# A hybrid decoder layer on one core: attention with a written order on the matmul engine

## The chip, the core and the metric

The kernel runs on one core of a Trainium2 chip. A core has five engines that run beside each other and meet through semaphores: PE (TensorE, matrix products into the accumulator PSUM; PEld is its loading of the stationary operand), DVE (VectorE), ACT (ScalarE), POOL (GpSimdE) and SP (SyncE, which here issues the DMAs). The metric is device time in microseconds (us) of one execution, lower is better.

## The reference

One layer: two mixers read the same normalized input, their outputs go through one output projection, and a convolutional feed-forward part follows. Cut to the mixer that the change touches:

```python
xn = rms_norm(h, mix_pre_g[l])
proj = xn @ w_in[l]                       # z | xbc | dt | q | k | v
...
y_ssd = ssd_mixer(z, xbc, dt_raw, ...)
y_sb = rms_norm(stick_breaking_attention(q, k, v).reshape(Bsz, L, SB_WIDTH), sb_norm_g[l])
mix = jnp.concatenate([y_ssd, y_sb], axis=-1) @ w_out[l]
h = h + rms_norm(mix, mix_post_g[l])
# feed-forward: up projection, causal convolution of 3, gelu gate, down projection

# stick_breaking_attention, for a block of 128 queries i of one head
zlog = jnp.einsum('bqhd,bkhd->bhqk', qi, kp) * scale
log_beta = jax.nn.log_sigmoid(zlog)
log_keep = jnp.where(valid, log_beta - zlog, 0.0)
after = lax.cumsum(log_keep, axis=3, reverse=True) - log_keep
w = jnp.where(valid, jnp.exp(log_beta + after), 0.0)
return jnp.einsum('bhqk,bkhd->bqhd', w, vp)
```

Sixteen heads of 64, 1024 tokens behind 16 learned meta tokens (L = 1040), model width 1024, all float32.

## The kernel before

The program goes through four stages: the SSD mixer (to about 440 us), attention (440 to 1048 us), the output projection with its norms, and the feed-forward part (from about 1205 us). The change is in the second.

**Attention** runs over eight pairs of heads (`p`) and, in each pair, eight blocks of 128 queries (`i`). A block of index i sees 16 + 128(i+1) keys, so its work grows with i. One block takes these steps, in this order of need:

- `block_weights`: the scores. PE multiplies q by k into PSUM (`z`, L577) in one piece for i up to 2, in two for i from 3 to 6 and in three for i = 7. ACT takes two sigmoids of each piece (`kp` L578, `bt` L579). DVE forms the running product along the keys by a scan, one for each head (L582). POOL multiplies it into `bt` (L584).
- `block_turn`: PE transposes the weights in `bt`, 128 keys at a time (`tw`, L598), into one PSUM tile, or two for i from 4 on. DVE masks the diagonal part and copies the first tile to SBUF (`th`, L602 and L605); ACT copies the second (L607).
- `block_mix`: PE multiplies `th` by the values v (`av`, L619); ACT puts the result away.

`z` and `tw` come from one ring of two PSUM tiles (tag `zz`, two buffers): a new `z` or `tw` has to wait until the tile two places earlier was read, by the sigmoids (of a `z`) or by the copies (of a `tw`). After each pair, `edge_turn` and `edge_mix` do the same for the 16 keys at the end of every block's range (`twc`, `thc`, `avc`).

Between the blocks PE has other work to fill in. `qkv_steps` projects the next pair's q, k and v: nine chains of 24 matmuls (`pj`, L164) in three column pieces, with operands split into a high and a low part, hence three matmuls for each of the eight slices of the model width. `post` then turns v (`vtp`, `vtc`). Once the projections are used up, in pairs 6 and 7, `wout_steps` loads and splits eight slices of the output weights (`wora`; ACT `woha` L705, DVE `wola` L706, and a small matmul `halo` L696 of each), and `ssd_half` multiplies the SSD result by them in 16 chains (`mo`, L747, `first` in the code). When attention has ended, the second half of the output weights (`worb`) is loaded in the same way beside what remains of those chains.

**What sets the order.** In attention the order of each engine's instructions is chosen by the framework's scheduler, which starts from the order of the code and its own estimate of when things are ready. The loop at the end of attention (L773 to L806) writes for a block: scores of block b, transposes of block b-1, one chain of projection, values of block b-1. An engine works through its own list strictly in that order, so an instruction whose input is late holds up all that stand behind it. DMAs stand in SP's list in the same way.

Of the kernel before, what the change touches and what calls it, by code (L numbers as in the profile page):

```python
# [16 lines left out]
P = 128  # L17
# [3 lines left out]
NM = 16  # L21
# [30 lines left out]
def tile_layer(ctx: ExitStack, tc: tile.TileContext, x, meta, rows, parts,  # L52
# [105 lines left out]
    def project_steps(w, ncol, xh, xl, chunks, evac, name):  # L158
        hi, lo = w
        for c0, n in chunks:  # L160
            acc = psum_mm(f"pj_{name}_{c0}")
            for k in range(KB):
                for j, (a, b) in enumerate(((hi, xh), (hi, xl), (lo, xh))):
                    mm(acc[:ncol, :n], a[:, k, :ncol], b[:, k, c0:c0 + n],  # L164
                       start=(k == 0 and j == 0), stop=(k == KB - 1 and j == 2))
            evac(acc, c0, n)
            yield
# [5 lines left out]
    def flow(items, lag=1):  # L173
        post = None
        for steps, after in items:
            for i, _ in enumerate(steps):
                if i == lag and post is not None:
                    post()
                    post = None
                yield  # L180
            if post is not None:
                post()
            post = after
        if post is not None:
            post()
# [47 lines left out]
    def qkv_steps(p):  # L233
        q = rp.tile([P, L + 3], F32, tag="rq", name=f"q{p}")
        k = rp.tile([P, L], F32, tag="rk", name=f"k{p}")
        for wsrc, dst, nm in ((w_q[p], q, "q"), (w_k[p], k, "k")):
# [3 lines left out]
            yield from project_steps(load_w(wsrc, P, f"{nm}{p}"), P, xh, xl, CH, ev, f"{nm}{p}")  # L240
# [8 lines left out]
        yield from project_steps(load_w(w_v[p], P, f"v{p}"), P, xh, xl, CH, evv, f"v{p}")  # L249

        def post():
            for part in range(2):
                tp = psum_tp(f"vtp{p}_{part}")
                for b in range(4):
                    c0 = (4 * part + b) * P
                    nc.tensor.transpose(tp[:, b, :], vt[:, c0:c0 + P], ident)
                nc.vector.tensor_copy(v[:, 4 * part:4 * part + 4, :], tp)
# [11 lines left out]
        posts[p] = post  # L269

    posts = {}

    def qkv_flow(p):
        return (qkv_steps(p), lambda: posts.pop(p)())
# [13 lines left out]
    with tc.tile_pool(name="ssd", bufs=1, side="right") as sp:  # L288
        def xbc_steps(b, dst, nm):
            raw = rp.tile([P, L + 3], F32, tag="rq", name=f"craw_{nm}")  # L290
# [25 lines left out]
        def bc_flow(g):  # L316
# [4 lines left out]
            return [(xbc_steps(8 + g, bt, f"B{g}"), lambda: to_tokens(bt, bn, f"B{g}")),  # L321
                    (xbc_steps(10 + g, ct, f"C{g}"), None)]

        def x_flow(g, b):
            xsT = rp.tile([P, L], F32, tag="rk", name=f"xsT{g}_{b}")
# [8 lines left out]
            return xbc_steps(4 * g + b, xsT, f"X{g}{b}"), post  # L334
# [10 lines left out]
        def xz_flow(g):  # L345
            for b in range(4):
                yield x_flow(g, b)
            for b in range(4):
                yield z_steps(g, b), None
# [38 lines left out]
        e, s, s2, q, adt = (t3(n, tdp) for n in ("e1", "s1", "s2", "q1", "adt"))  # L388
# [35 lines left out]
        bc[0][1]()  # L424
        run(fill)

        def chunk_weights(g, c):
# [25 lines left out]
            cbm = sp.tile([P, P], F32, tag="cbm", name=f"cbm{nm}", bufs=2)  # L453
# [81 lines left out]
        run(flow([x_flow(0, b) for b in range(2, 4)] + [(z_steps(0, b), None) for b in range(4)], 2))  # L535
# [5 lines left out]
        fill = flow(qkv_flow(p) for p in range(2))  # L541
# [20 lines left out]
    def block_weights(p, i):  # L562
# [10 lines left out]
        for ci, (a, w) in enumerate(chunks):  # L573
            z = psum_zz(f"z{nm}_{ci}")
# [11 lines left out]
        return p, i, bt  # L586
# [65 lines left out]
    def attend_meta():  # L652
        mv = ap.tile([P, 2, 4, P], F32, tag="th", name="meta_v", bufs=2)[:NM].rearrange("p h b c -> p (h b) c")
# [99 lines left out]
    def ssd_half(w):  # L753
        ys = [split_y(wp, 0, 1, ("whi", "wlo", WB))]
# [16 lines left out]
    later = flow(qkv_flow(p) for p in range(2, 8))  # L771
    meta_steps = attend_meta()
    for p in range(8):  # L773
        for i in range(NT):
            turn.append(block_weights(p, i))
            if len(turn) > 1:
                mix.append(block_turn(*turn.pop(0)))
            if p == 0:
                run(fill, 1)
            elif p < 7:  # L780
                run(later, 1 + (p < 7 and i == (0 if p == 6 else NT - 1)))
            else:
                if i == 0:
                    run(later)
                elif i < 4:
                    run(meta_steps, 1)
                run(first, (0, 0, 1, 1, 1, 2, 2, 2)[i])
            if mix:
                block_mix(*mix.pop(0))
            if p == 0 and i == 2:  # L790
                token_rstd(r_ssd, ap, "a")
            if p > 0 and i == 0:
                edge = edge_turn(p - 1)
            elif p > 0 and i == 1:
                edge_mix(p - 1, edge)
        if p == 0:
            run(fill)
        if p == 6:
            xpool.close()
            w1pool = wo1.enter_context(tc.tile_pool(name="wo1", bufs=1, side="left"))  # L800
            wres = []
            halo = psum_mm("halo0")
            run(wout_steps(w1pool, 0, ssd_g, wres, halo_y(w1pool, 0, ssd_g), halo))
            halo_store(w1pool, 0, halo)
            first = ssd_half(wres)
    while turn:  # L806
        block_mix(*block_turn(*turn.pop(0)))
    edge_mix(7, edge_turn(7))
    run(meta_steps)
    apool.close()  # L810
# [796 lines left out]
```

## Time and profile before

| what | value |
|---|---|
| median of 3 timed runs | 1871.89 us (1871.78 to 1872.38) |
| the profiled execution, its own time | 1875.09 us |
| its span from first to last instruction | 1873.4 us |
| DVE busy | 1100.6 us (59%) |
| ACT busy | 761.1 us (41%) |
| POOL busy | 854.6 us (46%) |

The profiled execution is one of its own, 3.2 us above the median; 1.7 us of its time lie outside the span. The busy time of an engine is the sum of its instructions' times in the span; PE's is shown below. The ends of matmuls are modelled by the profiler, so that a chain of matmuls overlaps itself in the rows. A window row gives, for one stretch, its length and each engine's busy time; the difference is the engine's idle time there.

### The profile page before, as it was taken

What the parts mean: (1) busy time and instruction counts of PE and PEld (TensorE: products, weight loads), DVE (VectorE), ACT (ScalarE), POOL (GpSimd) and SP (SyncE); (2) the same over time, 40 slices, a digit from 0 to 9 for tenths busy, and PEclk for the clock granted to TensorE, in tenths of its full rate; (3) what the DMA queues carried; (4) which work ended last, traced back from release to release, by engine and by line L of the source; (5) the groups of instructions that cost most, each with busy time, mean ns of one, the idle gap of its engine ahead of it and who ended that gap; (6) DMA issues with size and microseconds to landing.
All of it is one profiled execution on the core that took longest, in us unless ns stands there. A gap on an engine that the chain in (4) does not pass through costs nothing. (4 is left out here: it accounts for less than half of the span.)

```text
span 1873.4 us, 27435 instructions
## 1 busy us (share of the span) xinstructions
PE 1770.0 (94%) x10957; PEld 1509.8 (81%) x10957; DVE 1100.6 (59%) x1286; ACT 761.1 (41%) x1275; POOL 854.6 (46%) x614
## 2 busy tenths in 40 slices
PE   5899999999899999999889999899999999999997
PEld 4899889888678778778647677798988999888886
DVE  5551873674645445454533336767666666666888
ACT  5323553543343444443444234443333323334444
POOL 3213663485455554554434313248777777600001
PEclk9999999999999999999979999999999999999999
DMA  4123343131011011010042355323322323187334
GB/s 151 46 69 127 80 121 115 47 99 52 12 35 35 24 34 35 23 35 24 13 131 68 119 163 186 127 70 105 111 85 85 124 98 102 66 275 252 97 114 162
DMA packets 91443, 173.96 MB, mean 93 GB/s; under 512 B 11722, under 2 KB 36714, under 8 KB 91316
## 3 DMA queue, kind: packets, MB, share of 16 engines
q1 hardware_dynamic: 91316, 172.21, 29.0%
q8 instruction: 86, 1.41, 0.3%
q14 instruction: 41, 0.34, 0.1%
HBM read 122.39 MB, written 49.79 MB: 92 GB/s over the span
## 5 line engine op out<-in xcount | busy, mean ns | idle before, releaser
L584 POOL TENSOR_TENSOR bt<-bt,kp 128x256 f32<-128x256 f32 (+7 forms) x128 | 212.7, 1681 | 238.0 <-DVE kp L582 238.0
L582 DVE TENSOR_TENSOR_SCAN kp<-kp,hold 128x272 f32<-128x272 f32 (+7 forms) x128 | 175.4, 1409 | 182.2 <-ACT kp L578 110.1
L972 POOL TENSOR_TENSOR wl<-wr,wh 128x1024 fp32r<-128x1024 f32 x44 | 109.4, 2496 | 40.7 <-ACT wh L971 40.7
L1420 PE MATMUL dn<-dl,dh 128*128 128x512 f32 x308 | 119.9, 389 | 0.1
L1420 PE MATMUL dn<-dh 128*128 128x512 f32 x308 | 119.9, 389 | 0.0
L1420 PE MATMUL dn<-dh,dl 128*128 128x512 f32 x308 | 119.8, 389 | 0.0
L1466 POOL TENSOR_TENSOR fms<-fms,nhalf 128x1 f32<-128x1 f32 x8 | 8.5, 1061 | 225.8 <-DMA ar<-fda 186.0
L598 PE MATMUL tw<-ident,bt 128*128 128x128 f32 x576 | 82.2, 281 | 21.5 <-issue 13.9
L619 PE MATMUL av<-th,v 128*64 128x128 f32 x1152 | 81.4, 282 | 19.3 <-DVE th L605 19.2
L578 ACT ACTIVATE kp<-z 128x288 f32<-128x288 f32 (+6 forms) x112 | 82.8, 739 | 37.7 <-PE z L577 35.4
L598 PEld LDWEIGHTS tw<-ident,bt 128*128 128x128 f32 x576 | 63.4, 143 | 41.9 <-issue 28.0
L619 PEld LDWEIGHTS av<-th,v 128*64 128x64 f32 x1152 | 63.3, 138 | 39.6 <-DVE th L605 26.6
L1349 ACT ACTIVATE dh<-ar 128x512 fp32r<-128x512 f32 x77 | 48.7, 632 | 111.7 <-PE dn L1420 89.2
L971 ACT ACTIVATE wh<-wr 128x1024 fp32r<-128x1024 f32 x44 | 46.6, 1060 | 114.9 <-PE fX L1029 68.3
L1101 DVE SCALAR_TENSOR_TENSOR ga<-gr,pp,ga 128x1024 f32<-128x1024 f32 x44 | 71.3, 1621 | 34.8 <-ACT ga L1094 34.0
L577 PE MATMUL z<-k,q 64*128 64x144 f32 (+6 forms) x448 | 87.0, 489 | 3.2 <-ACT bt L579 3.2
L579 ACT ACTIVATE bt<-z 128x288 f32<-128x288 f32 (+6 forms) x112 | 83.1, 742 | 0.0
L1350 DVE TENSOR_TENSOR dl<-ar,dh 128x512 fp32r<-128x512 f32 x77 | 53.2, 691 | 42.0 <-ACT dh L1349 41.9
L1420 PEld LDWEIGHTS dn<-dl,dh 128*128 128x128 f32 x308 | 57.8, 188 | 12.5 <-DVE dl L1350 0.4
L1420 PEld LDWEIGHTS dn<-dh 128*128 128x128 f32 x308 | 57.8, 188 | 12.1 <-ACT dh L1349 0.3
L1420 PEld LDWEIGHTS dn<-dh,dl 128*128 128x128 f32 x308 | 57.8, 188 | 12.0
L164 PE MATMUL pj_v<-xh,wh_v 128*128 128x346 f32 (+1 forms) x192 | 65.5, 341 | 0.0
(545 smaller groups left out, 5797.4 us busy)
## 6 DMA issues: line engine op xcount, KB each, us to landing
wr<-in_w_up SPq DMA_DIRECT2D x44, 512.0 KB, 4.5
fds<-ga SPq DMA_DIRECT2D x44, 256.0 KB, 2.0
b<-in_w_down SPq DMA_DIRECT2D x44, 256.0 KB, 5.1
ar<-fds SPq DMA_DIRECT2D x44, 256.0 KB, 2.7
fda<-ga SPq DMA_DIRECT2D x33, 256.0 KB, 3.3
ar<-fda SPq DMA_DIRECT2D x33, 256.0 KB, 3.2
yk<-yd SPq DMA_DIRECT2D x16, 512.0 KB, 3.8
zd<-zt SPq DMA_DIRECT2D x8, 520.0 KB, 3.2
```

The source lines that it names most:

```text
L164: mm(acc[:ncol, :n], a[:, k, :ncol], b[:, k, c0:c0 + n], start=(k == 0 and j == 0), stop=(k == KB - 1 and j == 2))
L577: mm(z[:, j, :w], q[h, t0:t0 + P], k[h, a:a + w], start=True, stop=True)
L578: nc.scalar.activation(kp[:, :, a:a + w], z[:, :, :w], AF.Sigmoid, scale=-QSCALE)
L579: nc.scalar.activation(bt[:, :, a:a + w], z[:, :, :w], AF.Sigmoid, scale=QSCALE)
L582: nc.vector.tensor_tensor_scan(kp[:, j][:, ::-1], kp[:, j][:, ::-1], hold[:, L - n:L][:, ::-1], 1.0, op0=ALU.mult, op1=ALU.max)
L584: nc.gpsimd.tensor_tensor(bt[:, j, 0:m], bt[:, j, 0:m], kp[:, j, 1:m + 1], op=ALU.mult)
L598: nc.tensor.transpose(tw[:, j, b, :], bt[:, j, c0:c0 + P], ident)
L619: mm(av[halves[j], :], v[:, kb, halves[j]], th[:, j, b, :], start=kb == 0, stop=kb == i)
L972: nc.gpsimd.tensor_tensor(l, raw, h.bitcast(F32), op=ALU.subtract)
L1101: nc.vector.scalar_tensor_tensor(v, self.g[jj][:, :, i:i + 256], fconv_w[:, j, i:i + 1], v, op0=ALU.mult, op1=ALU.add)
L1350: sub(lo[:, k], raw, hi[:, k].bitcast(F32), op=ALU.subtract)
L1420: mm(banks[t], u[:, 0, c], v[:, 1, :], start=(p == 0 and i == 0), stop=(p == NPR - 1 and i == 2))
```

## The change

The order of PE's instructions in attention is now the order of the code (`manual_schedule` for PE alone); the other engines keep the scheduler. The loop over the blocks is rewritten for it:

- For block b the code writes: the first two pieces of its scores, one or two half chains of projection, its third piece if it has one, the values of block b-3, the transposes of block b-2, and another half chain. Before it was scores of b, transposes of b-1, a whole chain, values of b-1.
- A projection chain yields in its middle (`halves_`), so that one step is 12 matmuls and not 24. All eight pairs' projections come from one `flow`; a pair's weights are loaded one projection ahead (`weights_of`), and the three parts of `post` are spread over three steps.
- The edge products come at blocks 2 and 3 of the next pair, not 0 and 1.
- The projections end in pair 6, block 3. The loading of `wora` is spread over blocks from pair 6, block 5, two slices for a block, and the `mo` chains start in pair 7, block 2; 13 of 16 chains now stand ahead of the end of attention or right behind it, 9 before.
- Buffers: q and k three deep, `bt` three deep and not four, the mask tile `cbm` of the SSD scan one deep and not two, two temporaries of the SSD stage share memory with others, `meta_v` moved to another pool.

```diff
     def project_steps(w, ncol, xh, xl, chunks, evac, name, halves_=False):
...
             for k in range(KB):
+                if halves_ and k == KB // 2:
+                    yield
...
+    qkv_w = [(src[p], f"{nm}{p}") for p in range(8) for nm, src in (("q", w_q), ("k", w_k), ("v", w_v))]
+    ready = {}
+
+    def weights_of(name, ahead=0):
+        n = [nm for _, nm in qkv_w].index(name) + ahead
+        if n < len(qkv_w) and qkv_w[n][1] not in ready:
+            src, nm = qkv_w[n]
+            ready[nm] = load_w(src, P, nm)
+        return ready.get(name)
+
+    def qkv_block(name, evac, halves_):
+        w = weights_of(name)
+        for i, _ in enumerate(project_steps(w, P, xh, xl, CH, evac, name, halves_)):
+            if halves_ and i == 1:
+                weights_of(name, 1)
+            yield
...
+        post += [lambda: turn_v(0), lambda: turn_v(1), turn_edge]
...
-        btt = ap.tile([P, 2, L], F32, tag="bt", name=f"bt{nm}", bufs=4)
+        btt = ap.tile([P, 2, L], F32, tag="bt", name=f"bt{nm}", bufs=3)
...
         for ci, (a, w) in enumerate(chunks):
+            if ci == 2:
+                yield
             z = psum_zz(f"z{nm}_{ci}")
...
-        return p, i, bt
+        turn.append((p, i, bt))
...
+    pe_order = ExitStack()
+    pe_order.enter_context(tc.manual_schedule(engines={mybir.EngineType.PE}))
     for p in range(8):
         for i in range(NT):
-            turn.append(block_weights(p, i))
-            if len(turn) > 1:
-                mix.append(block_turn(*turn.pop(0)))
-            if p == 0:
+            if p == 0 and i == 0:
                 run(fill, 1)
-            elif p < 7:
-                run(later, 1 + (p < 7 and i == (0 if p == 6 else NT - 1)))
...
+            block = block_weights(p, i)
+            next(block, None)
+            if p > 0 and i == 3:
+                edge_mix(p - 1, edge)
+            run(fill, 1 + (i < 3))
+            run(first, int(p == 7 and i > 4))
+            run(block)
             if mix:
                 block_mix(*mix.pop(0))
+            if len(turn) > 2:
+                mix.append(block_turn(*turn.pop(0)))
+            run(fill, int(p > 0 or i > 3))
+            if p == 6 and i == 5:
+                run(fill)
+                xpool.close()
...
+                wsteps = wout_steps(w1pool, 0, ssd_g, wres, halo_y(w1pool, 0, ssd_g), halo)
+            if p == 7 and i == 1:
+                run(wsteps)
+                halo_store(w1pool, 0, halo)
+                first = ssd_half(wres, ys1)
+            elif p > 5:
+                run(wsteps, 2)
...
+            run(first, int(p == 7 and i > 1))
...
+            if p > 0 and i == 2:
                 edge = edge_turn(p - 1)
...
+    while turn or mix:
+        if mix:
+            block_mix(*mix.pop(0))
+        if turn:
+            mix.append(block_turn(*turn.pop(0)))
+        run(first, 1)
+    edge = edge_turn(7)
+    run(first, 1)
+    edge_mix(7, edge)
     run(meta_steps)
+    pe_order.close()
```

**What stands where.** PE before, pair 3, from the scores of block 6 to those of block 7 (a name's first number is the block, a second one the piece; matmuls of the projection are `pj`, of which two are shown and the others left out):

```order
L577 MATMUL z_6_0_6223<-k_5207,q_5206 128x456 x2
L577 MATMUL z_6_1_6228<-k_5207,q_5206 128x456 x2
L164 MATMUL pj_v_0_6266<-xh,wh_v_6261 128x348
L164 MATMUL pj_v_0_6266<-xl,wh_v_6261 128x348
L598 MATMUL tw_5_0_6238<-ident,bt_5_6151 128x128 x8
...
L598 MATMUL tw_5_1_6249<-ident,bt_5_6151 128x128 x4
...
L619 MATMUL av_5_6292<-th_5_0_6247,v_5634 64x128 x8
L619 MATMUL av_5_6292<-th_5_1_6254,v_5634 64x128 x4
L577 MATMUL z_7_0_6308<-k_5207,q_5206 128x348 x2
L577 MATMUL z_7_1_6313<-k_5207,q_5206 128x348 x2
```

The same place now, with twelve `pj` at each of the two marks:

```order
L599 MATMUL z_6_0_6337<-k_5029,q_5028 128x456 x2
L599 MATMUL z_6_1_6342<-k_5029,q_5028 128x456 x2
...
L282 MATMUL vtc_6368<-ident,edge_6365 128x128
L641 MATMUL av_3_6375<-th_3_0_6313,v_5429 64x128 x8
L620 MATMUL tw_4_0_6385<-ident,bt_4_6194 128x128 x8
L620 MATMUL tw_4_1_6396<-ident,bt_4_6194 128x128 x2
...
L599 MATMUL z_7_0_6416<-k_5029,q_5028 128x348 x2
L599 MATMUL z_7_1_6421<-k_5029,q_5028 128x348 x2
```

Transposes and values between the scores of blocks 6 and 7 are those of blocks 4 and 3 now, and were both those of block 5; the values no longer stand behind their own transposes.

DVE before, same pair (`kp` the scan of both heads, `th` the copy and the mask of a `tw`):

```order
L582 SCALAR_TENSOR_TENSOR kp_6_6221<-kp_6_6221,hold 128x912 x2
L605 COPY th_5_0_6247<-tw_5_0_6238 128x1024
L602 TENSOR_TENSOR th_5_1_6254<-tw_5_1_6249,late 128x2x128
L582 SCALAR_TENSOR_TENSOR kp_7_6306<-kp_7_6306,hold 128x1040 x2
L605 COPY th_6_0_6337<-tw_6_0_6328 128x1024
L602 TENSOR_TENSOR th_6_1_6346<-tw_6_1_6339,late 128x2x128
```

DVE now:

```order
L604 SCALAR_TENSOR_TENSOR kp_6_6335<-kp_6_6335,hold 128x912 x2
L283 COPY vc_6054<-vtc_6368 128x128
L627 COPY th_4_0_6394<-tw_4_0_6385 128x1024
L624 TENSOR_TENSOR th_4_1_6399<-tw_4_1_6396,late 128x2x128
L604 SCALAR_TENSOR_TENSOR kp_7_6414<-kp_7_6414,hold 128x1040 x2
L627 COPY th_5_0_6470<-tw_5_0_6461 128x1024
L624 TENSOR_TENSOR th_5_1_6477<-tw_5_1_6472,late 128x2x128
```

The copies are those of one block earlier than before, and still stand behind the scan of the block whose scores were last written. By the ring of two, `z_7_0` of the row above reuses the tile of `tw_4_0`, and `z_0_0` of the next pair that of `tw_5_0`: they wait for these copies. Before, it was `av_5` that waited for `th_5_0`.

DVE now at the handover from projections to output weights, pair 6, blocks 6 and 7:

```order
L627 COPY th_4_0_8222<-tw_4_0_8213 128x1024
L624 TENSOR_TENSOR th_4_1_8227<-tw_4_1_8224,late 128x2x128
L728 SCALAR_TENSOR_TENSOR wola_8232<-wora_8229,pp,woha_8231 128x1024
L728 SCALAR_TENSOR_TENSOR wola_8240<-wora_8237,pp,woha_8239 128x1024
L728 SCALAR_TENSOR_TENSOR wola_8301<-wora_8298,pp,woha_8300 128x1024
L604 SCALAR_TENSOR_TENSOR kp_7_8245<-kp_7_8245,hold 128x1040 x2
L627 COPY th_5_0_8288<-tw_5_0_8279 128x1024
L624 TENSOR_TENSOR th_5_1_8295<-tw_5_1_8290,late 128x2x128
L728 SCALAR_TENSOR_TENSOR wola_8309<-wora_8306,pp,woha_8308 128x1024
```

And PE there, block 7 and the start of pair 7:

```order
L718 MATMUL halo_8168<-wora_8229,y_8169 2x512 x2
L599 MATMUL z_7_0_8247<-k_6848,q_6847 128x348 x2
L599 MATMUL z_7_1_8252<-k_6848,q_6847 128x348 x2
L599 MATMUL z_7_2_8257<-k_6848,q_6847 128x344 x2
L641 MATMUL av_4_8267<-th_4_0_8222,v_7250 64x128 x8
L641 MATMUL av_4_8267<-th_4_1_8227,v_7250 64x128 x2
L620 MATMUL tw_5_0_8279<-ident,bt_5_8128 128x128 x8
L620 MATMUL tw_5_1_8290<-ident,bt_5_8128 128x128 x4
L718 MATMUL halo_8168<-wora_8237,y_8169 2x512 x2
L718 MATMUL halo_8168<-wora_8298,y_8169 2x512 x2
L599 MATMUL z_0_0_8318<-k_7455,q_7454 128x144 x2
```

From the last `pj` on, in pair 6, block 3, seven blocks stand on PE with nothing between them but the small `halo` matmuls and the turning of v, until the first `mo` chain in pair 7, block 2. Before, projections filled PE to the end of pair 6.

More of the change, by code (lines that the diff above doesn't have):

```diff
@@ L793, in tile_layer @@
                 edge = edge_turn(p - 1)
[L794 to L805, printed above, removed]
```

98 lines of the change are left out of this document (47 added, 51 removed).

## The prediction

> **What bounds the kernel now.** I read the page first: each engine's busy time and the clock strip.
>
> ```profile
> PE 1770.0 (94%) x10957; PEld 1509.8 (81%) x10957; DVE 1100.6 (59%) x1286; ACT 761.1 (41%) x1275; POOL 854.6 (46%) x614
> PEclk9999999999999999999979999999999999999999
> ```
>
> PE is busy 94% of the span and the next engine 59%, so the time is PE's work, plus its idle stretches, plus what a lower clock adds. The strip dips in one slice, in attention's second half. The change leaves the matmuls alone; it can only win or lose idle time and clock. So the windows view comes next, one row for each pair of heads and finer rows about the dip (columns: window, length, busy time and count of PE, PEld, DVE, ACT, POOL, granted clock, DMA share, GB/s).
>
> ```profile
> 440.60:507.90 67.30, 58.49 (x427) 47.08 (x426) 35.11 (x43) 27.66 (x47) 39.74 (x38) 0.99 0.09 28
> 507.90:572.80 64.90, 60.27 (x462) 49.40 (x460) 32.51 (x38) 29.39 (x51) 33.80 (x30) 0.98 0.08 26
> ...
> 643.90:715.00 71.10, 66.56 (x507) 55.22 (x505) 35.48 (x43) 29.95 (x52) 37.70 (x30) 1.00 0.10 31
> ...
> 786.10:857.40 71.30, 66.48 (x505) 55.17 (x503) 35.39 (x43) 29.95 (x52) 37.61 (x30) 1.00 0.10 31
> 857.40:930.30 72.90, 66.94 (x506) 55.37 (x503) 37.95 (x44) 27.66 (x50) 31.21 (x26) 1.00 0.05 16
> 930.30:953.80 23.50, 18.38 (x135) 8.60 (x131) 16.69 (x25) 13.05 (x20) 6.51 (x11) 1.00 0.47 141
> 953.80:974.30 20.50, 17.28 (x62) 10.99 (x63) 7.20 (x11) 10.29 (x20) 11.55 (x12) 0.50 0.31 101
> 974.30:985.40 11.10, 11.10 (x57) 8.58 (x57) 0.00 (x0) 3.49 (x6) 2.60 (x2) 1.00 0.41 138
> 985.40:1047.60 62.20, 60.18 (x379) 45.80 (x377) 24.23 (x20) 21.03 (x33) 26.84 (x15) 1.00 0.17 57
> 1047.60:1101.00 53.40, 49.58 (x219) 34.61 (x217) 16.05 (x13) 19.09 (x23) 10.50 (x4) 0.94 0.51 156
> ```
>
> A pair in the steady part (pairs 2 to 5; the third row shown is pair 3, the fourth pair 5) takes 71.1 us with PE idle for 4.5. Pair 0 is idle for 8.8. From 857.4 to 1047.6, where projections give way to output weights, the idle times are 6.0, 5.1, 3.2, 0 and 2.0, together 16.3. Of 17.28 us busy at clock 0.50, half, 8.6, is the price of the clock. What ends the idle time of pair 3 is in the waits view for PE in that window (us in total, times, longest):
>
> ```profile
> PE av L619 <- DVE th L605: 1.7, 3, 1.0
> PE tw L598 <- issue: 1.5, 3, 0.6
> PE tw L598 <- POOL wl_k L154: 0.8, 1, 0.8
> PE z L577 <- ACT bt L579: 0.5, 1, 0.5
> ```
>
> These are small stalls: values that wait for a copy, transposes that wait for sigmoids (the ring). They understate a little. The timeline shows a chain's matmuls starting 0.16 us apart:
>
> ```profile
> 639.71 0.32 PE L164 MATMUL pj_v<-xh,wh_v 128*128 128x346 f32 x1
> ...
> 641.62 0.32 PE L164 MATMUL pj_v<-xh,wh_v 128*128 128x346 f32 x1
> ...
> 641.94 0.32 PE L164 MATMUL pj_v<-xh,wl_v 128*128 128x346 f32 x1
> 642.19 1.75 PE L619 MATMUL av<-th,v 128*64 128x128 f32 x28
> ```
>
> Twelve starts take 1.91 us, though each is drawn 0.32 long, so a wait behind a `pj` hides a further 0.16 us. With eight such entries a pair loses 4.5 + 8 x 0.16 = 5.8 us. An unhindered switch costs 642.19 - 641.94 - 0.16 = 0.09, and a half chain with its two switches 2.1.
>
> **The change, pairs 1 to 5.** The values go from one block behind to three, so their wait for the copy of their own transposes, 1.7 us, goes. The transposes no longer stand a chain behind the scores. What is late next follows from the ring of two: the scores of block b+1 reuse the tiles that the transposes of b-2 filled, and the copy that frees these stands in DVE's list behind the scan of block b. So PE gets from scores to scores no faster than scores, sigmoids, scan, copy. The durations, PE's rows first, then a sigmoid of ACT and the rows of DVE:
>
> ```profile
> 679.82 1.09 PE L619 MATMUL av<-th,v 128*64 128x128 f32 x16 [0.17 <-DVE th L605]
> 680.84 1.59 PE L577 MATMUL z<-k,q 64*128 64x392 f32 x8
> ...
> 688.94 1.31 PE L619 MATMUL av<-th,v 128*64 128x128 f32 x20 [0.50 <-DVE th L605]
> 690.18 1.80 PE L577 MATMUL z<-k,q 64*128 64x456 f32 x8
> 693.25 1.07 PE L598 MATMUL tw<-ident,bt 128*128 128x128 f32 x8 [0.76 <-POOL wl_k L154]
> ...
> 700.72 1.44 PE L577 MATMUL z<-k,q 64*128 64x348 f32 x8
> 703.15 0.85 PE L577 MATMUL z<-k,q 64*128 64x344 f32 x4 [0.48 <-ACT bt L579]
> ```
>
> ```profile
> 704.24 0.78 ACT L578 ACTIVATE kp<-z 128x688 f32<-128x688 f32 x1
> ```
>
> ```profile
> 684.30 3.47 DVE L582 TENSOR_TENSOR_SCAN kp<-kp,hold 128x784 f32<-128x784 f32 x2 [4.54 <-issue]
> ...
> 694.08 4.01 DVE L582 TENSOR_TENSOR_SCAN kp<-kp,hold 128x912 f32<-128x912 f32 x2 [4.86 <-ACT kp L578]
> 698.00 1.20 DVE L605 COPY th<-tw 128x1024 f32<-128x1024 f32 x1
> ...
> 705.12 4.54 DVE L582 TENSOR_TENSOR_SCAN kp<-kp,hold 128x1040 f32<-128x1040 f32 x2 [5.59 <-ACT kp L578]
> ```
>
> - Block 6: scan 3.9 after its scores (690.18 to 694.08), then 3.9 to the copy (698.00), then 1.2: block 7's scores may start at +9.0. PE has meanwhile 1.7 of scores, two half chains of 2.1, values of 1.0 and transposes of 1.1, together 8.0. Wait 1.0.
> - Block 7: its third piece now follows a half chain, at 1.4 + 2.1 = +3.5. With 0.85 for it and 0.8 for its first sigmoid (the ACT row) the scan starts at +5.2, not at +4.4 (700.72 to 705.12). With 4.5 and 1.2 the next scores start at +10.9. PE has 1.4 + 2.1 + 0.8 + 1.2 + 1.2 + 2.1 = 8.8. Wait 2.1.
> - Block 5: +3.5, 3.5 and about 1.3 of copy and mask make 8.3 against 8.0. Wait 0.3.
> - The edge at block 2: 0.6, an estimate from its transpose and two mask operations. Blocks 0, 1, 3 and 4: PE has more than the chain.
>
> Sum 4.0, and 0.8 for eight more switches at 0.09: 4.8 us a pair, 5.8 before. **Five pairs win 5 us.** The bounds: nothing waits any more (5 x 5.0 = 25 won), or every copy comes 0.8 us later than reckoned at four blocks of a pair (16 lost, less the 5: 11 lost). I take the rows as they stand, since both chains are measured.
>
> **Pair 0.** Before: 8.8 idle, ten entries at 0.16, and about 1 us of low clock (0.99 of 67.3 us), together some 11. After, the same waits as above and 1.2 where block 3 has no second half chain, about 5. **Won: 6**, bounds 0 to 9.
>
> **The handover.** Before: 16.3 idle, 8.6 of clock, and 16 entries at 0.16: 27 us lost. After, seven blocks (pair 6 block 4 to pair 7 block 2) have no chain between. There a block lasts as long as its chain on ACT and DVE: about 6.9, 8.1, 9.0 and 10.1 for blocks 4 to 7, then some 5.5, 5.5 and 9 for the next pair's 0, 1 and 2 (estimates: shorter scans, but the edge and the split of output weights among them), together 54. The output weights interfere in DVE's list, where three `wola` stand ahead of block 7's scan.
>
> ```profile
> wora<-in_w_out SPq DMA_DIRECT2D x8, 512.0 KB, 3.8
> L705 ACT ACTIVATE woha<-wora,pp 128x1024 fp32r<-128x1024 f32 x8 | 9.1, 1146 | 0.7 <-DMA wora<-in_w_out 0.5
> L706 DVE SCALAR_TENSOR_TENSOR wola<-wora,pp,woha 128x1024 fp32r<-128x1024 f32 x8 | 10.4, 1303 | 2.0 <-ACT woha L705 2.0
> ```
>
> A slice takes 3.8 + 1.1 + 1.3 = 6.2 us and has two buffers, so the third `wola` comes up to a slice after the first two; I put 4 us on block 7's scan (bounds 0 and 6). That makes 58 us, with 35 of PE work: a pair without its projections is 71.1 - 5.8 - 34.5 = 31 us (nine chains of 24 at 0.16), of which seven of eight blocks are 28, plus 7 for `halo`, the turning of v and the first `mo`. Lost: 23, and 2.6 in the blocks on either side. The clock is the open price. It fell to 0.50 behind these two waits:
>
> ```profile
> 950.92 0.18 PE L671 MATMUL twm<-ident,btm 32*16 32x32 f32 x1 [1.45 <-POOL sq L650]
> 954.58 1.12 PE L619 MATMUL av<-th,v 128*64 128x128 f32 x8 [2.52 <-DVE th L605]
> ```
>
> The seven blocks leave PE idle about 3 us each, so half clock is to be expected there again. It hurts little where PE waits anyway: only the first scores and the sigmoids' start lie on the chain, about 1 us a block. Bounds 0 and 7, taken 4. After: 23 + 2.6 + 4 = 30. **Lost: 3**, bounds 5 won to 18 lost.
>
> [...]
>
> **The tail** (1047.6 to 1101.0). PE is idle 53.4 - 49.6 = 3.8 us there, one wait of `halo`. Its groups in this window (busy, mean ns, idle before):
>
> ```profile
> L747 PE MATMUL mo<-woha,yh 128*128 128x512 f32 x55 | 22.9, 416 | 0.0
> ...
> L696 PE MATMUL halo<-worb,y 128*2 128x512 f32 x32 | 7.0, 703 | 3.8 <-POOL yl L737 3.8
> ```
>
> This group is a third of seven chains (24 matmuls each); the three groups share PE in turn, and by the rule of their overlap (0.23 us from start to start, an estimate from 53.4 us less `halo`, idle and the edge over 168) a chain takes 5.5. Thirteen are done by then after the change, so three are left, not seven, to cover the second half of the weights. Its eight slices at 6.2 take 25 us if loads overlap splitting, 50 if they don't; PE has 3 x 5.5 + 7 = 24 beside them, and the first chains of the second half come slice by slice. I put 6 to 7 lost after, and before it is 3.8 idle and 3.2 of clock (0.94 of 53.4), 7 too: 0. Bounds: 4 won (no wait), or 50 - 24 - 11 = 15 lost, less the 7: 8 lost; 11 is another two drip-fed chains.
>
> **The rest at nothing.** Three buffers for q and k let projections run two ahead, and weights loaded one projection earlier move SP's loads forward where DMA is 10% busy. Three of `bt` and not four suffice, for a tile is read two blocks on. The single `cbm` and shared temporaries lie in the SSD stage, whose PE order is the same; if POOL's mask stalled there it would cost under 1 us a block, at most 4 in all.
>
> **Sum:** -5 - 6 + 3 + 0 = -8: 1875.1 to 1867.1 for the profiled execution, 1871.9 to **1864** for the median.
>
> **Rivals.**
> 1. The copies come in time, because DVE is half idle (35.5 of 71.1 us) and three blocks lie between, so the waits really go. For it: before, the scans waited 4.5 to 5.6 us for input, so an earlier sigmoid brings all forward. Against: the copy stands behind a scan that itself hangs on the newest scores. Pairs 1 to 5 win 25, pair 0 wins 9, handover and tail 0: **1838**.
> 2. Slower: the handover starves. Every output slice in DVE's or ACT's list ahead of a scan holds its block back by 4 us, as reckoned for one; if it does so at four blocks, that is 12 more, and half clock throughout adds 3. It decides once the seven blocks take over 74 us (62 forecast, 12 more for the 8 won and the 4 of the measurement). At 77: **1879**. For it: two slices a block need more than 6.2 us with two buffers, and blocks 0 and 1 are shorter than that. Against: DMA is far from full.
> 3. The stalls only change place: the z of each pair waits as long as `av` and `tw` did (5.8 a pair), pair 0 wins 4, the handover loses 4: **1872**. This is the change not doing what it says.
>
> **How the numbers follow.** Forecast 0.50 (its own range 1855 to 1871), rival 1 0.15, rival 2 0.18, rival 3 0.17. A measurement of this kernel can tell 0.2%, 3.7 us, from no change: the top of the forecast's range, 0.08, counts as same. Faster 0.42 + 0.15 = 0.57, same 0.17 + 0.08 = 0.25, slower 0.18. The range goes to rivals 1 and 2: 1838 to 1880.
>
> **What would show it.** Right: PE's waits in a pair are of `z` for DVE's `th` or scan, none of `av`; about 1 us ahead of block 7's scores and 2 ahead of the next pair's; a pair period near 70; the seven blocks near 62 us with a clock between 0.5 and 1. Wrong: a period under 67 (rival 1), the seven blocks over 74 (rival 2), the period unchanged (rival 3), a wait of over 15 us for `worb` in the tail, or a new idle stretch outside 440 to 1101, for which I reckon nothing.

## The result, and the profile after

| kernel | median us (lowest to highest) | ratio to before, 95% interval |
|---|---|---|
| before | 1871.84 (1871.71 to 1872.38) | |
| changed | 1882.52 (1880.58 to 1885.97) | 1.0059 [1.0041, 1.0076] |

The change makes the kernel 0.6% slower, 10.7 us, where 8 us of gain were forecast. Its four executions lie further apart, 5.4 us against 0.7, but that is no property of the change: beside the experiments the kernel before gave medians of 1873.8 to 1874.1 us, and single executions from 1871.2 to 1877.1. The profiled execution, 1880.6 us with a span of 1878.9, was the shortest of the four; that of before was 3.2 us above its median. Between the two traces the spans differ by 5.5 us only, and it is this part of the 10.7 that they can explain.

The page of the changed kernel, the rows on PE's busy time and on the clock:

```profile
PE 1773.9 (94%) x10957; PEld 1518.5 (81%) x10957; DVE 1122.8 (60%) x1286; ACT 760.8 (40%) x1275; POOL 853.8 (45%) x614
PEclk9999999999999999999899999999999999999999
```

PE has the same 10957 matmuls and is busy 3.9 us longer; idle time is 105.0 us of the span after and was 103.4. DVE, with the same 1286 instructions, is busy 22.2 us longer. Both are signs of slower instructions, not of more of them.

The windows view, cut at the first scores of each pair, then at the last projection (875.0 is the start of pair 6, 910.5 its block 4), at pair 7's block 3 (969.9), and to 1047.0:

```profile
441.20:498.10 56.90, 52.88 (x366) 43.51 (x365) 33.70 (x41) 26.36 (x44) 36.09 (x37) 1.00 0.12 34
498.10:575.90 77.80, 71.27 (x515) 59.33 (x515) 39.94 (x44) 30.19 (x52) 35.20 (x29) 0.96 0.09 28
575.90:648.70 72.80, 69.75 (x517) 58.74 (x517) 36.60 (x43) 31.29 (x53) 37.59 (x30) 0.98 0.10 30
648.70:724.90 76.20, 69.85 (x517) 58.38 (x517) 39.91 (x43) 30.02 (x53) 40.05 (x31) 0.97 0.12 36
724.90:799.40 74.50, 70.69 (x516) 59.51 (x516) 37.50 (x43) 30.71 (x53) 37.23 (x30) 0.96 0.09 29
799.40:875.00 75.60, 69.93 (x517) 58.08 (x517) 40.93 (x44) 29.16 (x51) 35.12 (x29) 0.98 0.07 22
875.00:910.50 35.50, 33.09 (x266) 28.32 (x266) 15.36 (x23) 13.50 (x25) 10.28 (x15) 1.00 0.06 16
910.50:969.90 59.40, 44.76 (x318) 28.34 (x317) 40.64 (x38) 31.81 (x52) 36.07 (x27) 0.86 0.25 82
969.90:1047.00 77.10, 75.33 (x463) 57.89 (x464) 28.53 (x29) 29.54 (x49) 37.48 (x26) 1.00 0.24 79
```

Pairs 1 to 5 are where the time went. The same five pairs as one window, first before, then after:

```profile
507.90:857.40 349.50, 326.40 (x2472) 270.19 (x2470) 174.33 (x206) 149.18 (x259) 184.18 (x146) 1.00 0.10 30
```

```profile
498.10:875.00 376.90, 351.49 (x2577) 294.04 (x2577) 194.87 (x213) 151.37 (x262) 185.19 (x145) 0.97 0.10 29
```

The changed order puts 105 more matmuls there (eight half chains and the turning of one v), which at 0.16 us are 16.8 of work that stood in other stages before. 376.9 - 349.5 - 16.8 = **10.6 us lost**. The idle time is 25.4 us, 23.1 before; the clock is 0.97 and was 1.00. The loss is thus for the most part clock: 0.03 of 376.9 is 11 us, at most 1.3 before (0.98 in pair 1).

What PE waits for, from 430 to 1110 us, the largest rows before and after:

```profile
PE av L619 <- DVE th L605: 19.2, 27, 2.5
PE tw L598 <- issue: 13.9, 26, 0.8
PE tw L598 <- POOL wl_k L154: 4.1, 5, 1.0
PE halo L696 <- POOL yl L737: 3.8, 1, 3.8
PE z L577 <- ACT bt L579: 3.2, 7, 0.5
```

```profile
PE z L599 <- DVE th L627: 37.8, 20, 4.0
PE vtp L274 <- DVE v L275: 3.7, 3, 2.1
PE z L599 <- DVE thc L653: 2.1, 7, 0.3
PE z L599 <- ACT bt L601: 1.6, 2, 1.3
```

The waits of `av` and `tw` are gone and scores wait for `th` instead. The sum of the shown rows is 44 us before and 45 after. What differs is their shape: 27 and 26 waits of 0.5 to 0.7 us on average became 20 of 1.9. And the clock fell to 0.50 behind the longest of these, those of 2.10 to 3.96 us, and behind some of the others. Around the start of pairs 3 and 4, PE's rows, then two windows:

```profile
648.65 0.85 PE L599 MATMUL z<-k,q 64*128 64x144 f32 x4 [2.00 <-DVE th L627]
...
724.89 0.85 PE L599 MATMUL z<-k,q 64*128 64x144 f32 x4 [3.72 <-DVE th L627]
```

```profile
648.60:652.00 3.40, 3.35 (x13) 3.07 (x14) 2.15 (x3) 1.39 (x4) 3.40 (x4) 0.50 0.00 0
...
723.70:730.50 6.80, 5.61 (x21) 5.34 (x22) 3.45 (x6) 1.56 (x4) 5.09 (x6) 0.50 0.00 0
```

Behind this wait of 2.00 us the clock was 0.50 for 3.4 us, behind the one of 3.72 us for 6.8.

The two waits differ because of DVE. Its scan of block 7, and POOL beside it, in pair 3 and in pair 4:

```profile
717.96 5.75 DVE L604 TENSOR_TENSOR_SCAN kp<-kp,hold 128x1040 f32<-128x1040 f32 x2 [5.46 <-ACT kp L600]
723.64 1.19 DVE L627 COPY th<-tw 128x1024 f32<-128x1024 f32 x1
...
793.69 4.54 DVE L604 TENSOR_TENSOR_SCAN kp<-kp,hold 128x1040 f32<-128x1040 f32 x2 [4.95 <-ACT kp L600]
798.14 1.20 DVE L627 COPY th<-tw 128x1024 f32<-128x1024 f32 x1
```

```profile
716.96 2.37 POOL L154 TENSOR_TENSOR wl_q<-wr_q,wh_q 128x1024 fp32r<-128x1024 f32 x1 [2.61 <-ACT wh_q L153]
...
790.75 2.37 POOL L154 TENSOR_TENSOR wl_q<-wr_q,wh_q 128x1024 fp32r<-128x1024 f32 x1
```

In pair 3 the weight split `wl_q` had begun 1.0 us ahead of the scan and ran to 719.33; the scan took 1.2 us longer than in pair 4, where the split ended before it began and the wait behind it was 1.98 us. That is 1.2 us more for 1.4 us of overlap. In both pairs the copy that releases the next pair's scores follows the scan at once (the transposes that it reads had ended at 719.3 and 795.5), and the scores follow the copy. In pair 1 it was not a scan but what the turning of v leaves on DVE, ahead of the copy that block 7's scores waited 2.97 us for:

```profile
558.61 0.66 DVE L275 COPY v<-vtp 128x512 f32<-128x512 f32 x1
559.19 2.81 DVE L285 COPY meta_q<-q 64x2 f32<-64x2 f32 x2
562.03 1.23 DVE L627 COPY th<-tw 128x1024 f32<-128x1024 f32 x1
```

Two copies of two elements a row took 2.81 us there. They ended at 560.27 and 562.00, and POOL's two `bt`, which ran from 556.90 on, at 560.25 and 561.97. With POOL idle they took 0.34 (in the kernel before, at 579.61). So it is not the split only: these copies, too, were longer beside an instruction of POOL that had begun first.

### The profile page after: what moved, and what is told of

It reads as the page before. It is cut to its first block, busy times and chain, and to the rows that moved or that the text cites. A ratio compares the mean times of both kernels' runs of the same rounds, so it can differ in the third digit from the quotient of the medians.

```text
span 1878.9 us, 27466 instructions
## 1 busy us (share of the span) xinstructions
PE 1773.9 (94%) x10957; PEld 1518.5 (81%) x10957; DVE 1122.8 (60%) x1286; ACT 760.8 (40%) x1275; POOL 853.8 (45%) x614
## 4 chain that ended last, share of the span: by engine, by line
PE 44%; DVE 5%; issue 2%; ACT 2%; POOL 1%; DMA 1%; POOLq 0%; ACTq 0%; SPq 0%; DVEq 0%
PE dn L1455 11%; PE fX L1064 9%; PE mo L769 6%; PE fY L1064 6%; PE fA L1064 6%; PE av L641 1%; PE z L599 1%; DVE kp L604 1%; PE tw L620 1%; PE pj_v L166 1%; DVE oxn L922 1%; DVE mb L913 0%; POOL bt L606 0%; PE halo L718 0%; PE pj_k L166 0%
## 5 line engine op out<-in xcount | busy, mean ns | idle before, releaser
L604 DVE TENSOR_TENSOR_SCAN kp<-kp,hold 128x272 f32<-128x272 f32 (+7 forms) x128 | 188.4, 1513 | 136.7 <-ACT kp L600 99.9
L599 PE MATMUL z<-k,q 64*128 64x144 f32 (+6 forms) x448 | 91.9, 507 | 41.5 <-DVE th L627 37.8
L599 PEld LDWEIGHTS z<-k,q 64*128 64x128 f32 x448 | 37.8, 193 | 75.3 <-DVE th L627 35.0
L627 DVE COPY th<-tw 128x1024 f32<-128x1024 f32 (+3 forms) x56 | 55.2, 986 | 62.7 <-PE tw L620 62.6
L166 PE MATMUL pj_q<-xh,wh_q 128*128 128x346 f32 (+1 forms) x192 | 68.8, 358 | 0.0
```

Source lines behind the costliest of these rows:

```text
L166: mm(acc[:ncol, :n], a[:, k, :ncol], b[:, k, c0:c0 + n], start=(k == 0 and j == 0), stop=(k == KB - 1 and j == 2))
L599: mm(z[:, j, :w], q[h, t0:t0 + P], k[h, a:a + w], start=True, stop=True)
L604: nc.vector.tensor_tensor_scan(kp[:, j][:, ::-1], kp[:, j][:, ::-1], hold[:, L - n:L][:, ::-1], 1.0, op0=ALU.mult, op1=ALU.max)
```

## The experiments

Three theories were tested. **A**: the scores wait for a copy that stands behind the newest block's scan on DVE. **B**: the scans, lengthened by POOL's weight splits, make it worse. **C**: the chain from scores to turned weights is too long in sum, and a wait filled at one place comes back at another. The clock's part was tested by itself. All kernels are edits of the changed one; the last column is the window from pair 1's first scores to pair 6's, with 2576 to 2578 matmuls in each, 60 more in the one marked *. In this column the kernel before would stand at 349.5 + 16.8 = 366.3.

| kernel | median us | ratio to before, 95% interval | pairs 1 to 5, us |
|---|---|---|---|
| changed, again | 1884.26 | 1.0054 [1.0039, 1.0069] | 372.7 |
| splits on DVE (e1) | 1872.14 | 0.9995 [0.9984, 1.0006] | 368.3 |
| copy ahead of scan (e2) | 1870.79 | 0.9988 [0.9979, 0.9997] | 358.6 |
| its control (e4) | 1897.99 | 1.0121 [1.0101, 1.0142] | 386.7 |
| moved half chain (e3) | 1864.59 | 0.9959 [0.9939, 0.9979] | 359.9 |
| e1 and e3 (e8) | 1859.60 | 0.9921 [0.9905, 0.9938] | 356.3 |
| more matmuls in the wait (e7) | 1878.39 | 1.0023 [1.0012, 1.0034] | 370.2* |
| e2, early edge (e5) | 1849.53 | 0.9871 [0.9856, 0.9886] | 342.2 |
| e5, early y0 (e6) | 1847.36 | 0.9859 [0.9844, 0.9874] | 342.3 |
| e5, shorter distance (e9) | 1875.57 | 1.0008 [0.9999, 1.0018] | 363.4 |
| changed, old distance (e10) | 1936.53 | 1.0334 [1.0318, 1.0349] | 385.5 |

**e1, the weight splits on DVE.**

```diff
-        nc.gpsimd.tensor_tensor(lo[:, :, :ncol], raw[:, :, :ncol],
+        split = nc.vector if name[0] in "qkv" and name[1:] > "1" else nc.gpsimd
+        split.tensor_tensor(lo[:, :, :ncol], raw[:, :, :ncol],
```

> The changed kernel with one edit: from pair 2 on the low part of each projection weight (wl) is split by DVE, no longer by POOL. In the changed kernel's trace DVE's scans in attention take 17.8 us longer than the shortest of their kind, and 4.4 us before the change; a good part of it stands beside a wl of POOL (2.4 us each). Theory A (the waits come from the copy of a turned tile that stands behind the scan of the newest block, whatever the scan's length): the scans lose about 7 us of excess, DVE gains about 1.2 us of its own for each of 18 splits, and the time stays within 3 us of the changed kernel's 1882.5. Theory B (scans slowed by the wl beside them are what made the change slower): the long waits ahead of the next pair's first scores in pairs 1 and 3 (3.0 and 3.7 us) fall to the 2.0 of the others, and the time falls by 6 or more, to 1876 or below.

10 us under the changed kernel: B's figure for the time. The pairs take 368.3 us and not 376.9, though DVE has 15 instructions more in them. So B holds for a good part of the loss (8.6 us of the pairs' window; 4.4 against the changed kernel's second profile, in the table's first row). B's figure for the waits did not come out: the longest of pairs 1 and 3 fell from 2.97 and 3.72 us to 2.30 and 2.64, not to 2.0. The scores wait for `th` as before, so A is untouched:

```profile
PE z L600 <- DVE th L628: 36.0, 21, 4.0
```

**e2 and e4, the copy ahead of the scan and its control.** e4 has the second line of this diff alone; e2 also writes the scan behind the turned block.

```diff
-    pe_order.enter_context(tc.manual_schedule(engines={mybir.EngineType.PE}))
+    pe_order.enter_context(tc.manual_schedule(engines={mybir.EngineType.PE, mybir.EngineType.DVE}))
...
         m = n - NM
+        yield
         for j in range(2):
             nc.vector.tensor_tensor_scan(
...
-            run(block)
+            if i == 7:
+                next(block)
             if mix:
                 block_mix(*mix.pop(0))
-            if len(turn) > 2:
+            if len(turn) > 1:
                 mix.append(block_turn(*turn.pop(0)))
+            run(block)
             run(fill, int(p > 0 or i > 3))
```

> The changed kernel with DVE's order in attention written out too, and the scan of block b written behind the transposes of block b-2 and their copies. PE's order is that of the changed kernel; on DVE the copies now stand ahead of the scan. Theory A: the scores no longer wait for DVE's th (37.8 us in 20 waits in the changed kernel), or by under 8 us; a pair takes about 68 us and not 75.5, the clock in the pairs is 1.00, and the time falls by 25 to 35 us, to 1848 to 1858. Theory B (slowed scans): nothing is gained beyond 5 us, since the scans stay beside the wl and the chain of scan and product stays as long. Theory C (the chain from scores to turned weights itself is too long for its distance): the wait moves to the transposes (tw for bt of POOL), of the same size, and the time stays at 1882.

> The control for the copy ahead of the scan: DVE's order in attention is written out as well, with the code as in the changed kernel, so the copy stands behind the scan, as there. Theory A: the waits of the scores for th stay at 35 to 40 us and the time within 5 us of 1882.5. If a written order on DVE is by itself what helps or hurts, it shows here in the same measure as in the run with the copy ahead.

The two differ in the scan's place on DVE alone (PE's order is the same in both traces and in that of the changed kernel), and by 27 us, the size that A gave. Neither figure itself came out: e4 was expected near the changed kernel and is 15 slower, with 23 us of waits for `th` and not 35 to 40, and e2 is 13 slower than its range. The first rows of PE's waits tell why, those of e2, then of e4:

```profile
PE vtc L282 <- DVE edge L280: 20.0, 5, 5.6
```

```profile
PE z L599 <- DVE th L627: 23.0, 14, 3.7
PE vtc L282 <- DVE edge L280: 22.9, 6, 5.8
```

In e2 the scores' wait for `th` is down to 0.2 us. But in both the order written on DVE puts the copies of v's edge directly ahead of their transpose, and PE waits for these.

**e5 and e6, the rest of that order.**

```diff
+        def take_edge():
+            edge = rp.tile([P, NT, NM], F32, tag="edge", name=f"edge{p}", bufs=1)
...
-        post += [lambda: turn_v(0), lambda: turn_v(1), turn_edge]
+        post += [lambda: (take_edge(), turn_v(0)), lambda: turn_v(1), turn_edge]
```

> The kernel with the copy ahead of the scan, and the two copies of v's edge written on DVE two half chains ahead of the transpose that reads them. In the run with the copy ahead the scores no longer waited for th, but the edge's transpose waited 20.0 us in 5 waits for these copies, which its written DVE order had put late. If that is all that this order cost, these waits go, the five steady pairs fall by 15 to 20 us, and the time goes from 1870.8 to 1850 to 1857. Rival: the edge copies then delay a copy or a scan on DVE, the wait moves to other instructions of PE, and the time stays above 1865.

> The same, and the load of y0 for the halo, with DVE's product on it, ten blocks earlier. In the run with the copy ahead the halo matmuls waited 6.6 us for that product and 7.1 us for loads of output weights. Expected: the 6.6 us go, and the time is 4 to 7 us under that of the run with the early edge. Rival: the block behind them waits for its own scan anyway, and nothing changes.

e6 adds `y0_ = halo_y(ap, 0, ssd_g)` at pair 6, block 1. e5 came out as expected, at 1849.5, just under its range. Its five pairs in one window:

```profile
498.10:840.30 342.20, 339.32 (x2576) 285.89 (x2575) 195.13 (x215) 151.05 (x263) 188.65 (x144) 1.00 0.11 32
```

PE is idle for 2.9 us in five pairs and the clock is 1.00 throughout: the work is that of the changed kernel (2577 matmuls there), in 34.7 us less. DVE is as busy as there (195.1 and 194.9 us), and its scans in attention are still 18.3 us longer than the shortest of their shapes (17.8 there), so what slows its instructions is still there; with the copies ahead of the scan PE hardly waits for it. e6 won 2.2 us instead of 4 to 7: 6.7 us of waiting for `y` went, and 2.1 of it came back in the wait for the output weights' DMA (6.9 to 9.0). **e6 beats both kernels, by 1.4% to the one before.**

**e3, the half chain moved to where PE waits, and e8, with e1.**

```diff
-            run(fill, 1 + (i < 3))
+            run(fill, 1 + (i < 3 and not (p > 0 and i == 0)))
...
-            run(fill, int(p > 0 or i > 3))
+            run(fill, int(p > 0 or i > 3) + (i == 7))
```

> The changed kernel with one half chain of projection (12 matmuls, 1.9 us) moved: block 7 has three, two of them behind its transposes, and block 0 of the next pair two and not three. Nothing else is touched. Theory A: the wait ahead of the next pair's first scores (2.0 to 3.7 us) is filled by this half chain, block 0 does not need it, and with the long wait the half clock of some 4 us a pair goes too: 2 us of wait and 1 to 2 of clock for each of six pairs, 12 to 20 us, to 1863 to 1870. Theory C (the chain on DVE and ACT is too long in sum, not at one place): the wait comes back ahead of block 1 or 2, and the time stays within 4 us of 1882.5.

> The moved half chain (1864.6, 18 under the changed kernel) and the weight splits on DVE (1872.1, 10 under it) in one kernel. If the two remove different losses (the wait ahead of a pair's first scores; the long scans of pairs 1 and 3), the sum is 28 and the time about 1855. If both shorten the same wait, the sum is little more than the larger one, 1861 to 1865.

e3 gained 18 us from the move of twelve matmuls a pair (its executions lie between 1859.8 and 1871.4): C falls, the wait did not come back ahead of blocks 1 and 2. e8 came between its two figures: it gained 23 of the 28 of a plain sum, 5 more than e3 alone, where e1 alone gained 10. The two losses are separate in part only, as far as e3's spread lets one tell.

**e7, matmuls that nobody reads, put into the wait.**

```diff
+            if 0 < p < 6 and i == 7:
+                jk = psum_mm(f"jk{p}")
+                for k in range(12):
+                    mm(jk[:, :346], xh[:, k % 8, :P], xl[:, k % 8, :346], start=k == 0, stop=k == 11)
```

> The changed kernel and, in pairs 1 to 5, twelve matmuls more in the form of a half chain (1.9 us) behind block 7's last half chain; their result is read by nobody, and nothing is left out. They stand where PE waits 2.0 to 3.7 us for the next pair's first scores. If the half clock behind these waits comes from their length, the low clock in the pairs shrinks (11 us of loss in pairs 1 to 5 of the changed kernel's trace), and the kernel gets faster by 3 to 8 us although it does more, to 1875 to 1880. If the low clock has another cause, the matmuls fit into the wait and the time stays at 1882.5, or rises by what does not fit, to 1884.

With sixty matmuls more the kernel is faster, 1.0023 against 1.0054 of the changed kernel, whose intervals do not meet. Its five pairs:

```profile
497.30:867.50 370.20, 354.00 (x2637) 297.18 (x2637) 195.40 (x213) 151.19 (x262) 185.09 (x145) 0.99 0.10 30
```

The clock is 0.99 and not 0.97. Of the five waits that the matmuls were put into, four of 2.0 us fell to 0.1 us or none and one of 3.7 to 1.83, and no low clock is left behind them. It is left behind the two longest of the others, 2.96 and 2.10 us. So in this run the low clock went with PE's waits. That their length decides and not their sum is not shown by it, since it shortened both; for that stands the kernel before, with 23.1 us of idle time in waits of at most 1.0 us and a clock of 1.00.

**e9 and e10, the distance.** e9 is e5 with transposes one block behind and values two (`if len(turn) > 0`). e10 is the changed kernel with both at block b-1, a half chain between them:

```diff
-            if mix:
-                block_mix(*mix.pop(0))
-            if len(turn) > 2:
+            if len(turn) > 1:
                 mix.append(block_turn(*turn.pop(0)))
             run(fill, int(p > 0 or i > 3))
+            if mix:
+                block_mix(*mix.pop(0))
```

> The kernel with the early edge (1849.5), with the transposes one block behind the scores and the values two, not two and three; the copies stay ahead of the scan on DVE. If the distance of the change is what its new DVE order needs (scan and POOL's product of block b-1 take longer than the scores and one half chain), PE waits ahead of each tw for bt, 1 to 3 us in the blocks from 4 on, and the time rises by 20 to 40 us, to 1870 to 1890. If the place of the copy is all that counts and the distance nothing, the time stays within 5 us of 1849.5.

> The changed kernel with the old distance: transposes and values both of block b-1, a half chain between them, PE's order written, DVE's left to the scheduler. If the longer distance of the change is worth nothing by itself (the waits only changed place, from av and tw to z), the time stays within 6 us of the changed kernel's. If the longer distance does win the waits of av, and the scores' wait is the price of something else, it rises by 10 or more. In both cases the waits of PE are of tw and av and not of z.

PE's largest wait in e9, then in e10:

```profile
PE tw L627 <- POOL bt L613: 24.4, 17, 3.6
```

```profile
PE av L641 <- DVE th L627: 63.4, 36, 4.1
```

My theory that the distance is worth nothing by itself falls: with a half chain as the only cover, the old distance costs 52 us more than the new. Of these only 13 lie in pairs 1 to 5 (385.5 and 372.7 us in the table, with equal matmuls); 28 lie behind them, above all in pairs 6 and 7, where no projections are left to cover anything. The kernel before did without the distance because its scheduler put nearly a whole chain between `tw` and `av`; a written order of half chains cannot. And e9, 26 us behind e5, shows that the copy's place needs the distance as well: one block closer, PE waits for POOL's product.

**Again**, the changed kernel beside e9 and e10:

> The changed kernel once more, beside the two others on the same chip, for comparison: 1880 to 1886, low clock in the pairs again behind waits of 2 us and more, at places that differ somewhat from the first profile.

It gave 1884.3, and its five pairs 372.7 us where the first profile had 376.9, with the same instructions and nearly the same waits. But the clock was at 0.50 for 13.7 us of them, and in the first for 23.9. Ahead of pair 3 the wait is 1.99 us (2.00 there), and the clock behind it stays at 1.00; the four score matmuls take 0.52 us, at half clock they took 0.85:

```profile
646.67 0.52 PE L599 MATMUL z<-k,q 64*128 64x144 f32 x4 [1.99 <-DVE th L627]
```

```profile
646.60:650.00 3.40, 3.33 (x22) 3.19 (x23) 2.21 (x4) 1.34 (x4) 3.40 (x4) 1.00 0.00 0
```

How much the low clock costs thus differs between executions of one kernel by some 5 us.

## Why the prediction was wrong

- **What bounds it**: right. PE's work is the same in both traces; the time moved with its waits and its clock.
- **Waits change place from `av` and `tw` to `z`**: right, and so are their sizes where nothing disturbs them. Pairs 2 and 4 are idle for 3.05 and 3.8 us, 4.0 forecast; ahead of pair 3 stands 2.0, forecast 2.1. That is about the gain of 1 us a pair that was reckoned (4.5 idle before). That `tw` had waited for sigmoids, as the prediction reads its `issue` row, is not shown: the row names no releaser.
- **The first step that failed** is "I take the rows as they stand, since both chains are measured". They were measured where nothing else on DVE or POOL met them. In the changed order something does: in pair 3 the split beside the scan, in pair 1 the small copies ahead of `th`, and the idle time there is 6.4 and 6.5 us, about 3 more than in pairs 2 and 4; in pair 5 a wait for the copy of v takes 2.1. My bound for this (11 lost) held the result, the chosen value did not. The prediction costed the earlier weight loads at nothing by looking at DMA alone; POOL's split of these weights was left out, and so were the copies that come with the turning of v. In the five pairs PE was idle for 25.4 us, 20 forecast. e1 prices the split: about 10 us, the clock behind the longer waits among it. The copies by themselves were not tried.
- **The second step that failed**, and the larger: the clock in pairs 1 to 5 was left at 1.00. I gave the low clock a price at the handover only, though the rows that I quoted for it were waits of 1.45 and 2.52 us, and my own sum had put a wait of 2.1 into each pair. With nearly the same idle time in the five pairs, 23.1 and 25.4 us, the clock was 1.00 where no wait was over 1.0 us and 0.97 where the longest was 3.72. Size: some 10 us in this trace, 6 to 7 in the second (half of 13.7); e7 won 4 to 6 us by filling the waits. Forecast for the five pairs: 5 won; measured: 10.6 lost. The pair period, named as near 70 us, was 75.4; 3.4 of it are the half chains that moved in, on which the prediction said nothing.
- **Pair 0**: 6 won forecast; idle 8.8 to 4.0 us and clock 0.99 to 1.00 are 5.5.
- **The handover**: its seven blocks took 59.4 us (910.5 to 969.9), 62 forecast. That this came so near is luck: PE was idle for 14.6 us there, 23 forecast, and the clock cost 0.14 x 59.4 = 8.3, 4 forecast with a bound of 7. From 875.0 to 1047.0 idle time and clock are 18.8 and 8.3 us, together 27; the same two were 16.3 and 8.6 before, 25. So 2 lost, 3 forecast. Rival 2, for which the slower side was kept, did not occur; the loss came in the pairs.
- **The tail**: 0 forecast, some 4 us lost. From 1047.0 to 1258.1 idle time is 14.8 us and the clock costs 6.3; before, from 1047.6 to 1252.6, they were 12.6 and 4.7. (From there on both kernels have 620.8 us left.) The loss lies in the later part, outside the stretch to 1101 for which the prediction reckoned, before and after:

```profile
1101.00:1252.60 151.60, 142.86 (x745) 121.75 (x745) 96.27 (x112) 63.96 (x100) 53.84 (x37) 0.99 0.42 142
```

```profile
1105.00:1258.10 153.10, 139.73 (x714) 117.12 (x713) 97.44 (x112) 66.54 (x105) 50.40 (x36) 0.97 0.42 139
```

Here a wait of `x2tp` for DVE is 3.9 us and was 1.6; why is open. No wait for `worb` is over 0.6 us.
- **Rival 3** (the waits only change place) was the nearest, and its 1872 lacks the clock. Idle time and clock by stage do not add up to the 5.5 us between the spans; that the rest are waits hidden behind a `pj`, which are in no row, is the author's estimate.

On the clock: the row of 2.00 us ahead of pair 3 was enough for a clock of 0.50 in the first trace, and of the 23.9 us at half clock in pairs 1 to 5 13.7 stand behind waits of 1.88 to 2.10 us.

## What to carry to other kernels

Order an engine together with the one that frees its buffers: moving PE's readers two blocks back lost 10 us while the copy that frees the ring still stood behind the newest scan on DVE, and gained 24 when it stood ahead and v's edge was copied early (e5). Judge idle time of PE by the length of each wait, not by its sum (here 23.1 us in waits of at most 1.0 us went with a clock of 1.00, 25.4 us in waits of up to 3.72 us with 0.97), and put the filler where the longest waits are, here those of about 2 us and more. When loads or copies move, follow what they meet on every engine, here POOL's splits and products beside DVE's scans and copies (5.75 us for two scans beside a split, 4.54 without it).

## What the runs showed of the hardware

In pairs 1 to 5 of five traces (both of the changed kernel, e1, e3 and e7) every wait of PE of 2.10 us or more was followed by a clock of 0.50, and of those between 1.8 and 2.06 us only some: in the first trace those of 1.88, 2.00 and 2.01, not those of 1.98 and 2.06 nor the one of 2.00 ahead of pair 6. The kernel before has one of 1.75 us with half clock behind it (at 505.5 us). So the length alone does not decide. Nor does it set how long the low clock lasts: in the two traces of the changed kernel each such stretch in attention is 3.41 us or twice that, and a wait of 3.96 us was followed by 6.83 in the first and by 3.41 in the second. And not every stretch has a wait ahead of it: in the second trace the clock is 0.50 from 458.1 to 461.5 us, and in the 20 us before that PE has no wait of over 0.1 us.

DVE's scans took longer beside an instruction of POOL that had begun ahead of them: 5.75 us for the two scans of block 7 in pair 3 and not 4.54, with 1.37 us of overlap with `wl_q`. Of the 17.8 us by which the changed kernel's scans in attention exceed the shortest of their shapes, 8.0 stand beside a split `wl` and 7.5 beside the last `bt` of the pair before, which begins 0.5 to 0.9 us ahead of a new pair's first scan. No wait of PE follows these. In pair 2, and in the kernel before for comparison:

```profile
572.69 5.79 POOL L606 TENSOR_TENSOR bt<-bt,kp 128x1024 f32<-128x1024 f32 x2 [10.52 <-DVE kp L604]
```

```profile
576.99 2.15 DVE L604 TENSOR_TENSOR_SCAN kp<-kp,hold 128x144 f32<-128x144 f32 x2 [0.81 <-ACT kp L600]
```

```profile
574.48 0.79 DVE L582 TENSOR_TENSOR_SCAN kp<-kp,hold 128x144 f32<-128x144 f32 x2
```

The 8.0 and 7.5 us are those of fourteen scans. They overlap with the `wl` or the `bt` by 0.58 to 1.76 us, and each is longer than the shortest of its shape by 0.1 us less than its own overlap (0.47 to 1.65 us). A `bt` that begins after the scan of the other head did not lengthen that (at 796.44 in pair 4, with 4.54 us for the two scans).
